# Two mixed layers on one core: a new order for the last group of the MLP, two transposes put inside other products, a halved last sigmoid, and gate sums one call earlier

## The chip, the cores and the metric

The kernel runs on one core of one Trainium2 chip. The metric is the device time of one execution in microseconds. The engines of the core work side by side, each through its own list of instructions in a fixed order: TensorE (PE in the profile; PEld is its weight load) does matrix products and transposes into PSUM banks, VectorE (DVE) and ScalarE (ACT) do elementwise work, GpSimd (POOL) does next to nothing here, and SyncE (SP) issues nearly all transfers between HBM and the on-chip memory; ScalarE's queue issues a few.

## The reference

A trunk of two layers on x of 512 tokens by 1024. Layer 0 mixes tokens with a Mamba-2 SSD block, layer 1 with HGRN2. What this text is about is the second half of each layer, which is the same in both:

```python
h = layer_norm(DEEPNORM_ALPHA * x + mix, ln_g[i, 0], ln_b[i, 0])
h = layer_norm(DEEPNORM_ALPHA * h + sq_relu_mlp(h, mlp_w1[i], mlp_w2[i]), ln_g[i, 1], ln_b[i, 1])
x = h + jax.nn.sigmoid(h @ ple_w_gate[i]) * (p[i] @ ple_w_proj[i])

def sq_relu_mlp(h, w1, w2):          # 1024 -> 4096 -> 1024
    a = jax.nn.relu(h @ w1)
    return (a * a) @ w2
```

`p[i]` is a 512 by 256 embedding of the layer, `ple_w_proj[i]` takes it to 1024, and the gate is a 1024 by 1024 product. All numbers are fp32.

## The kernel before

Each fp32 product is made of three matmuls (`mm3`, lines 120 to 122): every operand is split into a high part (a cast by ScalarE, tags `whi` for weights) and a low part (the rest, a subtraction by VectorE, `wlo`), and high x high, high x low and low x high are summed in PSUM. A weight of 128 by 1024 is loaded by SP into one of three `raw` buffers (`unit`), then split into one of six `whi` and six `wlo` buffers (`split`: L114 is the cast, L116 the subtraction).

`mlp_and_gate(layer, ...)` is the second half of a layer. It has two parts.

**The MLP** runs in five groups. A group g below 4 makes eight tiles T of the hidden layer, 128 hidden features each (`hidden`: 24 matmuls into a bank `pj`, then ReLU, L528, and a square of two tiles together, L530, into z tiles of the tags `a` and `b`). After every fourth tile `half_blocks` makes from them half of the contents of seven operands, `a11`, `a12`, `a22`, `s1` to `s4`: a cast by ScalarE (L357), a low half by VectorE (L358), and four sums and differences between them (L362 to L366). These seven are the left factors of a 2 by 2 block product in seven products instead of eight (`block_product`). So the second matrix of group g - 1 is applied in seven products Q of 24 matmuls while the tiles of group g are made. The order within groups is written by hand, one string for each group:

```python
PERIODS = ("TTTTTTTT",) + 3 * ("TTQTQTQTQTQTQTQ",) + ("QQQQQQQ",)
for op in period:
    next(tiles if op == "T" else products)
    if 0 < g < 4 and op == "Q":
        next(ahead, None)
```

The products of groups 1 to 3 come in the order a11, a12, s2, s3, s1, a22, s4; those of the last group, which works on the blocks of group 3, in the order a11, s3, s2, a22, s1, a12, s4, so that the first two token chunks (`c` 0 and 1) are complete after s1. The right factors for s1, s2, s3 and a22 are sums of weights, made by `weight_sums` in eight buffers `r`; those for the others come through `raw`. `s3` and `s4` have two buffers of the tag `blk`, the other five share nine of the tag `b8`. A product of 24 matmuls adds its two banks (`py` or `pj`) into `acc` by VectorE (L471, in the last group for some L467, which sums up the row for the norm too).

**The sums of the gate's weights** are made ahead, during groups 1 to 3 (`sums_ahead`): 20 pieces in four rounds of five. A round loads four blocks of 256 KB into one `whi` and one `wlo` buffer, makes four sums in two pieces, then casts and subtracts in two more, and writes the results to HBM (`pre`) from ScalarE's queue: the high parts from `sg` (L418), the low parts, which stand in the `whi` and `wlo` buffers themselves, from there (L425). The writes of low parts of a piece are issued at the next call. One call (`next(ahead)`) is made after each product.

**The end of the layer.** The norm of a chunk (`chunk`) is followed by `turned(c)`: eight transposes on TensorE into the banks `pt` and `pm` (L318), and copies from there by ScalarE (L308, L324, L326) with low halves by VectorE (L309), which are the left factors of the gate's product. `turned(0)` is put behind the last matmul of the MLP's last product (`turns` in `block_product`), `turned(1)` behind the first embedding product, `proj(0, 0)`, six matmuls of p by `ple_w_proj`; `proj(1, 0)` follows. The gate is again a block product in seven parts. `finish(c, h, sg)` multiplies the sigmoid by the embedding product (L611), adds it into `acc` (L612), both on VectorE, and in layer 1 writes the output (L614). The very last `finish` works on two halves of 256 columns; its sigmoid (L673) is one instruction of 512 columns.

**What sets the order of instructions.** In this part of the program a planner lays out each engine's list from the program's order, priorities (`tc.high_priority(offset=n)` lets instructions pass for n places earlier in the program) and its own estimate of when operands are ready; TensorE's matmuls of different products may so be interleaved. `tc.issue_after(ins)` (here `behind`) keeps instructions behind one that is named, on the same engine. Once laid out, an engine takes its list strictly in order, and an instruction that waits holds all that stand behind it.

Of the kernel before, what the change touches and what calls it, by code (L numbers as in the profile page):

```python
# [11 lines left out]
AF = mybir.ActivationFunctionType  # L12
# [16 lines left out]
SOON = 40  # L29
TURN = 200  # L30

PERIODS = ("TTTTTTTT",) + 3 * ("TTQTQTQTQTQTQTQ",) + ("QQQQQQQ",)
SUMS = (60, 300, 300, 300)

JOBS = "q0 q1 v0 q2 q3 g0 q4 q5 v1 q6 q7 g1 o".split()
# [6 lines left out]
def trunk(ctx: ExitStack, tc, a):  # L42
    nc = tc.nc
# [14 lines left out]
    uid, marks = [0], {}  # L58
# [41 lines left out]
    def behind(ins):  # L100
        return nullcontext() if ins is None else tc.issue_after(ins.ins)
# [17 lines left out]
    def mm3(out, sh, sl, mh, ml, start, stop, **kw):  # L119
        nc.tensor.matmul(out, sh, mh, start=start, stop=False, **kw)  # L120
        nc.tensor.matmul(out, sh, ml, start=False, stop=False, **kw)  # L121
        marks["pe"] = nc.tensor.matmul(out, sl, mh, start=False, stop=stop, **kw)  # L122
# [36 lines left out]
    with tc.high_priority(offset=FIRST):  # L159
# [7 lines left out]
        for k in range(8):  # L167
            hi, lo = (v[:, k % 4, :] for v in early[k // 4])
            x, w = slots[k][:, 0:T], slots[k][:, T:768]
# [266 lines left out]
            us.append((hi, lo))  # L436
        return us

    def block_product(w, blk, lead, first, after=None, turns=None, sums=None):

        with behind(marks.pop(("turned", 0), None) if first else None):
            t1, t2, t3, t4 = weight_sums(w, lead)
        seen = set() if first else {(i, j) for i in range(2) for j in range(2)}
        banks = {}

        def product(x, f, name, start, i, j, turns=None):
            us = [split(v) if f in (t1, t2, t3, t4) else unit(v) for v in f]
            if start:  # L450
                banks[name] = [bank(psy, "py%d" % c) if name == "x" else bank(psj, "pj") for c in range(2)]
            t = blk[x]
            for c in range(2):
                ps = banks[name][c]
                sl = slice(c * P, (c + 1) * P)
                for k in range(4):
                    hi, lo = us[k // 2]
                    ks = slice((k % 2) * 512, (k % 2 + 1) * 512)
                    w_ = hi[:, ks], lo[:, ks]
                    mm3(ps, t[:, 0, k, sl], t[:, 1, k, sl], *w_, start and k == 0, k == 3, skip_group_check=True)  # L460
                    if turns and (c, k) == (1, 3):
                        with behind(marks["pe"]):
                            turns()
                d = acc[:, 2 - 2 * i + c, j * 512 : (j + 1) * 512]
                with tc.high_priority(offset=SOON if after else 0):
                    if after and f in (w[1][0], t1, t4, w[1][1]):
                        marks["acc"] = nc.vector.tensor_tensor_reduce(  # L467
                            d, ps, d, 1.0, 0.0, ALU.add, ALU.add, sums[:, 2 - 2 * i + c, j : j + 1]
                        )
                    elif (i, j) in seen:  # L470
                        marks["acc"] = nc.vector.tensor_add(d, ps, d)  # L471
                    else:
                        marks["acc"] = nc.vector.scalar_tensor_tensor(d, d, ALPHA, ps, ALU.mult, ALU.add)
            seen.add((i, j))

        p1 = lambda: product("a11", w[0][0], "x", True, 0, 0)
        p2 = lambda: product("a12", w[1][0], "z", True, 0, 0)
        p6 = lambda: product("s2", t2, "x", False, 1, 0)
        p7 = lambda: product("s3", t3, "y", True, 1, 1)
        p5 = lambda: product("s1", t1, "x", False, 1, 1)  # L480
        p4 = lambda: product("a22", t4, "y", False, 1, 0)
        p3 = lambda: product("s4", w[1][1], "x", False, 0, 1, turns)
        for f in (p1, p7, p6, p4, p5, p2, p3) if after else (p1, p2, p6, p7, p5, p4, p3):
            f()
            if after and f is p5:
                after(0), after(1)
            if after and f is p3:
                after(2), after(3)
            yield

    def mlp_and_gate(layer, h_s, last, turns=()):

        w1, w2 = a[f"w1_{layer}"], a[f"w2_{layer}"]
        blocks = {}
# [44 lines left out]

        for g, period in enumerate(PERIODS):  # L540
            if g < 4:
                tiles = hidden(g)
            if g > 0:
                if g == 4:
                    blk, after, turned, sums, later = norm_blocks(2 * layer + 1)
                    p_s = (mk(w4, [P, 2, T], "a", F32R), mk(w4, [P, 2, T], "b", F32R))
                    praw = mk(raws, [P, 1024], "raw")
                    nc.sync.dma_start(praw, a[f"pT_{layer}"].rearrange("p k t -> p (k t)"))
                    praw = praw.rearrange("p (k t) -> p k t", k=2)
                    nc.scalar.copy(p_s[0], praw)  # L550
                    nc.vector.tensor_sub(p_s[1], praw, f32(p_s[0]))
                w = [[[w2[8 * g - 8 + 4 * i + 2 * j + u] for u in range(2)] for j in range(2)] for i in range(2)]
                products = block_product(w, blocks.pop(g - 1), SUMS[g - 1], g == 1, *((after, lambda: turned(0), sums) if g == 4 else ()))
            for op in period:
                next(tiles if op == "T" else products)
                if 0 < g < 4 and op == "Q":
                    next(ahead, None)
                if g == 4:
                    for _ in ahead:
                        pass  # L560
# [14 lines left out]

        pus, pps, held = {}, {}, {}

        def proj(c, h, parts=1):
            if h not in pus:
                pus[h] = unit(a[f"wp_{layer}"][h])  # L580
            pu = pus[h]
            pps[c, h] = []
            n = 512 // parts
            for i in range(parts):
                pp = bank(psj, "pj")[:, :n]
                for k in range(2):
                    ks = slice(k * 512 + i * n, k * 512 + (i + 1) * n)
                    mm3(pp, p_s[0][:, k, c * P : (c + 1) * P], p_s[1][:, k, c * P : (c + 1) * P], pu[0][:, ks], pu[1][:, ks], k == 0, k == 1)
                pps[c, h].append(pp)

        def product(x, f, c, ps, start, hook=()):
            cs = slice(c * P, (c + 1) * P)
            for k in range(4):
                hi, lo = f[k // 2]
                ks = slice((k % 2) * 512, (k % 2 + 1) * 512)
                mm3(ps, blk[x][:, 0, k, cs], blk[x][:, 1, k, cs], hi[:, ks], lo[:, ks], start and k == 0, k == 3, skip_group_check=True)
                for at in hook:
                    if (c, k) == at[:2]:
                        with behind(marks["pe"]):
                            turned(at[2])  # L600

        def finish(c, h, sg):
            with behind(marks["pe"]):
                while late:
                    late.pop(0)()
            pp = pps.pop((c, h))
            n = 512 // len(pp)
            for i, part in enumerate(pp):
                cs = slice(i * n, (i + 1) * n)
                d = acc[:, c, h * 512 + i * n : h * 512 + (i + 1) * n]  # L610
                nc.vector.tensor_mul(sg[:, cs], part, sg[:, cs])  # L611
                nc.vector.tensor_add(d, sg[:, cs], d)  # L612
                if last:
                    nc.sync.dma_start(a["out"][c * P : (c + 1) * P, h * 512 + i * n : h * 512 + (i + 1) * n], d)  # L614
            if not last:
                late.append(lambda: turn(h, c))

        two = lambda p, tag: [bank(p, tag % c if "%" in tag else tag) for c in range(2)]
        proj(0, 0)
        with behind(marks["pe"]):  # L620
            turned(1)
        proj(1, 0)
        xb = two(psy, "py%d")
        f = [unit(v) for v in wb[0][0]]
        for c in range(2):
# [3 lines left out]
        f = [unit(v) for v in wb[1][0]]  # L629
        for c in range(2):  # L630
            z = bank(psj, "pj")
            product("a12", f, c, z, True, ((1, 0, 2), (1, 3, 3)))
            sg = held[c]
# [4 lines left out]
        f = ready(pre, 2)  # L638
# [9 lines left out]
        f = ready(pre, 1)  # L648
# [4 lines left out]
        f = ready(pre, 3)  # L653
# [5 lines left out]
        f = ready(pre, 0)  # L659
# [7 lines left out]
        f = [unit(v) for v in wb[1][1]]  # L667
        for c in range(2):
            if c == 0:
                proj(0, 1)  # L670
            product("s4", f, c, xb[c], False)
            sg = tmp("sg", [P, T])
            nc.scalar.activation(sg, xb[c], AF.Sigmoid)  # L673
            if c:
                proj(1, 1, 2 if last else 1)
            finish(c, 1, sg)
        return x_n, late

# [3 lines left out]
    first = [bank(psy, "py0"), bank(psy, "py1")]  # L682
    for k in range(8):
        if k == 6:
            for i in range(8):
                for c in range(NCH):
# [4 lines left out]
                        start=i == 0,  # L691
# [3 lines left out]
        parts = [tuple(v[:, k % 4, i * P : (i + 1) * P] for v in early[k // 4]) for i in range(2)]  # L695
# [794 lines left out]
```

## Time and profile before

| | |
|---|---|
| median of 3 runs | 1412.51 us (1411.73 to 1412.81) |
| profiled execution | 1411.54 us |
| its span, first to last instruction | 1409.8 us |
| PE busy, PEld busy | 1400.4 us (99%), 1168.9 us (83%) |
| DVE, ACT, POOL busy | 1076.0 us (76%), 777.6 us (55%), 1.8 us |
| granted TensorE clock | 1.000 |

Matmuls are pipelined and their ends are modelled, so the busy time of PE hides short stops; a stop is better seen from the start of one matmul to the start of the next, or from the length of stretches of equal work. In a row such as `654.86 0.33 ACTq L425 ...` the first number is the start in us from the span's start, the second the duration; `L425` is the line of the kernel; `out<-in` gives the buffers' tags; what stands in brackets is the idle time of the engine before the instruction and what ended it. `ACTq` and `SPq` are issues of transfers by ScalarE and SyncE. In rows of stretches the columns are named in the header: length, then busy time and number of instructions for each engine, the granted clock (1.00 is full), the busy share of the DMA engines and GB/s.

### The profile page before, as it was taken

The numbers are of one execution on the slowest core, as the hardware profiler recorded it, in microseconds if no ns is written. First come the engines' busy times: TensorE is split into PE (matmuls) and PEld (weight loads), VectorE is DVE, ScalarE is ACT, GpSimd is POOL, SyncE is SP. The second block draws the span as 40 slices with busy tenths as digits, with TensorE's granted clock in tenths as the row PEclk, the third lists the DMA queues.
The fourth block names the chain that finished last, engine by engine and source line by source line (L and its number), as shares of the span: only waits on it lengthen the run. The fifth ranks groups of instructions, "written<-read, shape, count | busy, mean of one in ns | idle before, by whom it ended". The sixth has DMA issues, their size and how long they took to land.

```text
span 1409.8 us, 20492 instructions
## 1 busy us (share of the span) xinstructions
PE 1400.4 (99%) x7973; PEld 1168.9 (83%) x7973; DVE 1076.0 (76%) x1777; ACT 777.6 (55%) x1164; POOL 1.8 (0%) x11
## 2 busy tenths in 40 slices
PE   9999999999999999999999999999999999999998
PEld 7888888888988888887888888888898888888787
DVE  7997877696866878787985774776785877868986
ACT  7886666573554555545564446465454554544563
POOL 0000000000000000000000000000000000000000
PEclk9999999999999999999999999999999999999999
DMA  8423333323354646655473321222163566565364
GB/s 295 157 98 135 103 108 120 105 90 105 129 185 143 228 161 204 211 176 177 139 280 122 104 92 62 89 92 75 61 239 122 171 209 214 175 215 194 108 246 154
DMA packets 66819, 214.70 MB, mean 152 GB/s; under 512 B 7713, under 2 KB 8353, under 8 KB 66593
## 3 DMA queue, kind: packets, MB, share of 16 engines
q1 hardware_dynamic: 57504, 196.59, 41.6%
q10 hardware_dynamic: 9216, 16.78, 3.3%
q8 instruction: 63, 1.03, 0.3%
q14 instruction: 36, 0.29, 0.1%
HBM read 194.41 MB, written 18.94 MB: 151 GB/s over the span
## 4 chain that ended last, share of the span: by engine, by line
PE 96%; DMA 1%; DVE 1%; ACT 1%; issue 1%; SPq 0%; DVEq 0%; ACTq 0%
PE pj L120 25%; PE pj L122 24%; PE pj L121 24%; PE py L120 5%; PE py L122 5%; PE py L121 5%; PE py L881 1%; PE py L1147 1%; PE py L883 1%; DVE wlo L116 1%; PE pt L864 0%; DMA raw<-in_whvg 0%; DMA acc<-in_xw 0%; ACT whi L114 0%; DMA pre<-whi 0%
## 5 line engine op out<-in xcount | busy, mean ns | idle before, releaser
L116 DVE TENSOR_TENSOR wlo<-raw,whi 128x1024 fp32r<-128x1024 f32 x222 | 269.4, 1221 | 171.6 <-ACT whi L114 170.4
L114 ACT CAST whi<-raw 128x1024 fp32r<-128x1024 f32 x222 | 232.8, 1051 | 302.3 <-PE pj L121 157.5
L120 PE MATMUL pj<-b,whi 128*128 128x512 f32 (+1 forms) x1000 | 379.6, 380 | 0.0
L121 PE MATMUL pj<-b,whi 128*128 128x512 f32 (+1 forms) x1000 | 377.3, 377 | 0.0
L122 PE MATMUL pj<-b,wlo 128*128 128x512 f32 (+1 forms) x1000 | 377.3, 377 | 0.0
L122 PEld LDWEIGHTS pj<-b,wlo 128*128 128x128 f32 x1000 | 188.2, 188 | 34.8
L121 PEld LDWEIGHTS pj<-b,whi 128*128 128x128 f32 x1000 | 188.2, 188 | 34.2
L120 PEld LDWEIGHTS pj<-b,whi 128*128 128x128 f32 x1000 | 188.0, 188 | 34.1
L122 PE MATMUL pj<-whi,b 128*128 128x512 f32 x530 | 206.1, 389 | 0.0
L120 PE MATMUL pj<-whi,b 128*128 128x512 f32 x496 | 196.1, 396 | 0.0
L121 PE MATMUL pj<-wlo,b 128*128 128x512 f32 x496 | 193.2, 390 | 0.0
L114 ACT CAST whi<-r 128x1024 fp32r<-128x1024 f32 x64 | 67.2, 1053 | 96.6 <-PE pj L121 79.9
L122 PEld LDWEIGHTS pj<-whi,b 128*128 128x128 f32 x530 | 99.5, 188 | 20.7 <-DVE b L1342 0.2
L120 PEld LDWEIGHTS pj<-whi,b 128*128 128x128 f32 x496 | 93.2, 188 | 20.3 <-ACT k L1076 0.5
L121 PEld LDWEIGHTS pj<-wlo,b 128*128 128x128 f32 x496 | 93.2, 188 | 18.5
L120 PE MATMUL py<-whi,b 128*128 128x512 f32 x256 | 100.7, 393 | 3.1 <-ACT b L357 3.1
L122 PE MATMUL py<-whi,b 128*128 128x512 f32 x256 | 99.8, 390 | 0.0
L121 PE MATMUL py<-wlo,b 128*128 128x512 f32 x256 | 99.7, 389 | 0.0
L116 DVE TENSOR_TENSOR wlo<-r,whi 128x1024 fp32r<-128x1024 f32 x64 | 77.8, 1220 | 27.8 <-ACT whi L114 24.0
L120 PEld LDWEIGHTS py<-whi,b 128*128 128x128 f32 x256 | 48.0, 188 | 15.0 <-ACT b L357 3.9
L122 PEld LDWEIGHTS py<-whi,b 128*128 128x128 f32 x256 | 48.1, 188 | 10.1
L121 PEld LDWEIGHTS py<-wlo,b 128*128 128x128 f32 x256 | 48.1, 188 | 9.7
(374 smaller groups left out, 1934.1 us busy)
## 6 DMA issues: line engine op xcount, KB each, us to landing
raw<-in_w SPq DMA_DIRECT2D x112, 512.0 KB, 3.4
r<-in_w SPq DMA_DIRECT2D x64, 512.0 KB, 4.0
raw<-in_wssd SPq DMA_DIRECT2D x38, 512.0 KB, 3.6
a<-csd SPq DMA_DIRECT2D x16, 512.0 KB, 3.6
raw<-in_wso SPq DMA_DIRECT2D x16, 512.0 KB, 3.7
pre<-sg ACTq DMA_DIRECT2D x32, 256.0 KB, 3.0
whi<-pre SPq DMA_DIRECT2D x16, 512.0 KB, 5.3
wlo<-pre SPq DMA_DIRECT2D x16, 512.0 KB, 6.6
```

What stands on the lines that cost most here:

```text
L114: nc.scalar.copy(hi[:, :n], f)
L116: nc.vector.tensor_sub(lo[:, :n], f, f32(hi[:, :n]))
L120: nc.tensor.matmul(out, sh, mh, start=start, stop=False, **kw)
L121: nc.tensor.matmul(out, sh, ml, start=False, stop=False, **kw)
L122: marks["pe"] = nc.tensor.matmul(out, sl, mh, start=False, stop=stop, **kw)
L881: nc.tensor.matmul(yd[64 * r : 64 * r + 64, sl], xdt[:, c, r, :], m[:, r, sl], start=True, stop=c == 0)
L883: nc.tensor.matmul(yd[64 * r : 64 * r + 64, sl], pv[:, c - 1, r, :], ecs[:, r, (c - 1) * P : c * P], start=False, stop=True,)
L1147: nc.tensor.matmul(ps[r][32 * b : 32 * b + 32, base + n * c : base + n * c + n], kk[r][:, ts], moving(r, 4 * c + b), start=True, stop=True,)
```

## The change

- Group 3 is ordered `TTTQTQTQTQTQTQQ` instead of `TTQTQTQTQTQTQTQ`: three tiles come ahead of the first product, and the last two products stand together at the end, so the last tile comes ahead of the sixth product.
- In groups 1 to 3 one more call of `sums_ahead` is made, after the second tile of the group.
- `turned(0)` is issued after the third of the six matmuls of `proj(0, 0)`, and `turned(1)` after the third of `proj(1, 0)`; the parameter `turns` of `block_product` goes.
- The last sigmoid of layer 1 is made in two halves.
- The first half of the very last `finish` is added by GpSimd instead of VectorE. All other `finish` have one part and stay on VectorE.

```diff
-PERIODS = ("TTTTTTTT",) + 3 * ("TTQTQTQTQTQTQTQ",) + ("QQQQQQQ",)
+PERIODS = ("TTTTTTTT",) + 2 * ("TTQTQTQTQTQTQTQ",) + ("TTTQTQTQTQTQTQQ", "QQQQQQQ")
...
-                    if turns and (c, k) == (1, 3):
-                        with behind(marks["pe"]):
-                            turns()
...
-            for op in period:
+            for n, op in enumerate(period):
                 next(tiles if op == "T" else products)
-                if 0 < g < 4 and op == "Q":
+                if 0 < g < 4 and (op == "Q" or n == 1):
                     next(ahead, None)
...
-        def proj(c, h, parts=1):
+        def proj(c, h, parts=1, turn=None):
...
                     mm3(pp, p_s[0][:, k, c * P : (c + 1) * P], p_s[1][:, k, c * P : (c + 1) * P], pu[0][:, ks], pu[1][:, ks], k == 0, k == 1)
+                    if turn == c and k == 0:
+                        with behind(marks["pe"]):
+                            turned(c)
...
-                nc.vector.tensor_add(d, sg[:, cs], d)
+                (nc.vector if i == len(pp) - 1 else nc.gpsimd).tensor_add(d, sg[:, cs], d)
...
-        proj(0, 0)
-        with behind(marks["pe"]):
-            turned(1)
-        proj(1, 0)
+        proj(0, 0, turn=0)
+        proj(1, 0, turn=1)
...
-            nc.scalar.activation(sg, xb[c], AF.Sigmoid)
+            parts = 2 if last and c else 1
+            for i in range(parts):
+                cs = slice(i * 512 // parts, (i + 1) * 512 // parts)
+                nc.scalar.activation(sg[:, cs], xb[c][:, cs], AF.Sigmoid)
             if c:
-                proj(1, 1, 2 if last else 1)
+                proj(1, 1, parts)
             finish(c, 1, sg)
```

More of the change, by code (lines that the diff above doesn't have):

```diff
@@ L437, in ready, with block_product @@
         return us
-    def block_product(w, blk, lead, first, after=None, turns=None, sums=None):
+    def block_product(w, blk, lead, first, after=None, sums=None):
         with behind(marks.pop(("turned", 0), None) if first else None):
@@ L446, in block_product, with product @@
         banks = {}
-        def product(x, f, name, start, i, j, turns=None):
+        def product(x, f, name, start, i, j):
             us = [split(v) if f in (t1, t2, t3, t4) else unit(v) for v in f]
@@ L481, in block_product @@
         p4 = lambda: product("a22", t4, "y", False, 1, 0)
-        p3 = lambda: product("s4", w[1][1], "x", False, 0, 1, turns)
+        p3 = lambda: product("s4", w[1][1], "x", False, 0, 1)
         for f in (p1, p7, p6, p4, p5, p2, p3) if after else (p1, p2, p6, p7, p5, p4, p3):
@@ L552, in mlp_and_gate @@
                 w = [[[w2[8 * g - 8 + 4 * i + 2 * j + u] for u in range(2)] for j in range(2)] for i in range(2)]
-                products = block_product(w, blocks.pop(g - 1), SUMS[g - 1], g == 1, *((after, lambda: turned(0), sums) if g == 4 else ()))
-            for op in period:
+                products = block_product(w, blocks.pop(g - 1), SUMS[g - 1], g == 1, *((after, sums) if g == 4 else ()))
+            for n, op in enumerate(period):
                 next(tiles if op == "T" else products)
-                if 0 < g < 4 and op == "Q":
+                if 0 < g < 4 and (op == "Q" or n == 1):
                     next(ahead, None)
```

## The prediction

> **What bounds the kernel now.** I read the page first (busy shares), then the waits of TensorE, then equal stretches of the span beside each other, and last the instructions of ScalarE and VectorE in the two stretches that came out long.
>
> ```profile
> span 1409.8 us, 20492 instructions
> PE 1400.4 (99%) x7973; PEld 1168.9 (83%) x7973; DVE 1076.0 (76%) x1777; ACT 777.6 (55%) x1164; POOL 1.8 (0%) x11
> ```
>
> TensorE is the bound, and the change takes no matmul away. It can win only where TensorE stands still. Its waits by line:
>
> ```profile
> engine line waited for: us in total, times, longest us
> PE py L120 <- ACT b L357: 3.1, 2, 1.8
> PE pt L318 <- ACT b L324: 0.3, 1, 0.3
> ```
>
> L357 is the `copy` of `half_blocks`; its two waits, one in each layer, are what this change can reach, with L318 (`turned`); the list's other rows belong to the start of the program and to the next phase. Since matmul ends are modelled, I measure the loss by stretches of equal work. Rows 1 and 3: six tiles or products of 24 matmuls in the middle of group 3 of each layer. Rows 2 and 4: the six products from the last one of group 3 to the fifth of the last group.
>
> ```profile
> core 0: us, PE busy (x) PEld busy (x) DVE busy (x) ACT busy (x) POOL busy (x), PEclk, DMA share, GB/s
> 600.03:632.67 32.64, 32.64 (x146) 27.03 (x144) 27.68 (x31) 15.30 (x19) 0.00 (x0) 1.00 0.53 172
> 654.43:689.24 34.81, 33.58 (x146) 26.69 (x145) 29.75 (x41) 20.35 (x25) 0.00 (x0) 1.00 0.35 112
> 1251.98:1284.62 32.64, 32.64 (x145) 27.04 (x144) 27.58 (x31) 15.29 (x19) 0.00 (x0) 1.00 0.52 173
> 1306.38:1341.75 35.37, 33.50 (x146) 26.70 (x144) 30.32 (x42) 20.35 (x25) 0.00 (x0) 1.00 0.37 120
> ```
>
> The same 144 matmuls (the rest are neighbours cut by the edges) take 32.64 us undisturbed, so one operation of 24 takes 5.44 us and one matmul 0.227. The boundary loses 34.81 - 32.64 = 2.17 us in layer 0 and 35.37 - 32.64 = 2.73 in layer 1: 4.90 us together, at a granted clock of 1.00 in all four.
>
> Where it comes from, ScalarE and its own DMA issues, layer 0, then layer 1:
>
> ```profile
> 654.86 0.33 ACTq L425 DMA_DIRECT2D pre<-whi  x1
> 655.36 0.59 ACT L528 ACTIVATE b<-pj 128x512 f32<-128x512 f32 x1
> 655.98 1.06 ACT L530 ACTIVATE b<-b 128x1024 f32<-128x1024 f32 x1
> 658.96 2.00 ACT L114 CAST whi<-r 128x1024 fp32r<-128x1024 f32 x2 [1.92 <-DMA pre<-whi]
> 665.98 0.62 ACT L357 CAST b<-b 128x512 fp32r<-128x512 f32 x1 [2.51 <-DVE b L362]
> ...
> 1307.44 0.33 ACTq L425 DMA_DIRECT2D pre<-whi  x1
> 1311.53 2.00 ACT L114 CAST whi<-r 128x1024 fp32r<-128x1024 f32 x2 [2.54 <-DMA pre<-whi]
> ```
>
> The last tile T8 of group 3 is squared by 655.98 + 1.06 = 657.04. The next cast in ScalarE's order wants a `whi` buffer that the last piece of the gate sums is still writing to `pre`, and stands 1.92 us (2.54 in layer 1); the casts of T8's blocks are queued behind it, VectorE's low halves behind them. The `s3` block's second half comes out last:
>
> ```profile
> 668.27 0.68 DVE L358 TENSOR_TENSOR blk<-a,blk 128x512 fp32r<-128x512 f32 x1
> ...
> 1320.84 0.69 DVE L358 TENSOR_TENSOR blk<-a,blk 128x512 fp32r<-128x512 f32 x1
> ...
> 666.70 0.47 PE L120 MATMUL py<-whi,b 128*128 128x512 f32 x1 [1.23 <-ACT b L357]
> ```
>
> Without a stall, product a11 of the last group starts at 654.43 + 5.44 = 659.87, s3 at 665.31, and its second half of k six matmuls later, 666.67. Its low half is written at 668.95: 2.28 us late, against 2.17 lost. Layer 1: wanted at 1306.38 + 10.88 + 1.36 = 1318.62, written at 1321.53: 2.91 late, 2.73 lost. So the loss is the lateness of T8's blocks; the jumping ahead to ready halves of k (the 666.70 row) doesn't save it.
>
> **The change, part by part.**
>
> *The order of group 3.* Nothing is added. T8 changes places with the sixth product, so one more product, 5.44 us, stands between T8 and the s3 product. Against that: after T8, VectorE has that product's two accumulations more (2 x 0.69 = 1.4; an `acc<-py,acc` add is as long as the 0.69 row above), and its weights' casts come later. 5.44 - 2.28 - 1.4 = 1.8 us spare in layer 0, 1.1 in layer 1, before the hold is counted. The cover is the product itself; without it we are back at the loss. At the front of the group the first product waits for one more tile, whose blocks are older by then; the gate for `b8` buffers (`s2` of group 3 takes the one that `a11` of group 2 leaves) opens right before the fourth tile instead of before the third, and is wanted only after it. Weights on SP: two products in a row ask for two pairs of loads where a tile's single one stood between. The pair for Q6 is the `r` sums, the pair for Q7 `raw`; each is issued several operations ahead, so I take nothing. Ends: all of -4.90 to 0.
>
> *One more piece of the gate sums.* The generator has 20 pieces and a rest that only issues the last writes. Before, the rest came at the 21st call, at the last product of group 3: exactly the 654.86 write. With a call more in each group (8, 8, then) it comes at the fourth product of group 3, operation 10 of 15 instead of 15, and with it 4 loads of 256 KB on SP for each of the four rounds, the casts, VectorE's subtractions and ScalarE's writes. The hold of 1.92 and 2.54 leaves the boundary. That alone would leave 2.28 - 1.92 = 0.4 us late; with the other part, spare is 1.8 + 1.9 = 3.7 us, and 1.1 + 2.5 = 3.6 in layer 1. The price is paid elsewhere: the third round's writes move from the second product of group 3 to the last one of group 2, in front of the three tiles. Has such a hold cost TensorE anything elsewhere?
>
> ```profile
> 484.71 2.00 ACT L114 CAST whi<-raw 128x1024 fp32r<-128x1024 f32 x2 [2.85 <-DMA pre<-whi]
> 1137.36 2.00 ACT L114 CAST whi<-raw 128x1024 fp32r<-128x1024 f32 x2 [3.54 <-DMA pre<-wlo]
> 480.00:500.00 20.00, 20.00 (x90) 16.57 (x89) 15.28 (x20) 12.77 (x17) 0.00 (x0) 1.00 0.62 207
> 1130.00:1150.00 20.00, 20.00 (x90) 16.54 (x89) 15.79 (x20) 11.29 (x15) 0.00 (x0) 1.00 0.73 238
> ```
>
> Holds of 2.85 and 3.54 us, longer than those that hurt, and the 20 us around each hold 90 matmuls: 20 / 0.227 = 88 and the edges. Six weight buffers carry TensorE over them when no fresh block is wanted. Three tiles want none. Together these two edits: -4.90, which I take whole.
>
> *The turns.* `turned(0)` goes 3 matmuls (0.68 us) later, into the first embedding product; `turned(1)` into the second after its third matmul: six matmuls between the two now by program, nine in the trace. No instruction is added. What sets `turned(1)`:
>
> ```profile
> 700.76 0.58 ACT L308 CAST b<-pt 128x512 fp32r<-128x512 f32 x1 [4.83 <-PE pt L318]
> 701.92 1.05 ACT L114 CAST whi<-raw 128x1024 fp32r<-128x1024 f32 x1 [0.58 <-DMA raw<-in_wg]
> 702.88 0.58 ACT L324 COPY b<-pt 128x512 f32<-128x512 f32 x1
> 703.51 0.66 PE L318 MATMUL pt<-cst,acc 128*128 128x128 f32 x4 [0.26 <-ACT b L324]
> ```
>
> It needs the bank that L324 empties, and that copy stands behind a weight cast that waits for its load. `turned(0)` later makes L308 and so L324 later by up to 0.68; three matmuls remain to fill in. Ends: -0.3 (the wait gone) to +1.36 (0.68 shown in each layer). I take +0.4, nearer the first end, because the planner already puts embedding matmuls into that hole.
>
> *The tail.* VectorE's last four, ScalarE's last sigmoid, and the only rows that POOL and the output queue offer:
>
> ```profile
> 1404.36 0.60 ACT L673 ACTIVATE sg<-py 128x512 f32<-128x512 f32 x1 [2.12 <-PE py L122]
> 1405.14 0.42 DVE L611 TENSOR_TENSOR sg<-pj,sg 128x256 f32<-128x256 f32 x1 [1.46 <-PE pj L122]
> 1405.60 0.42 DVE L612 TENSOR_TENSOR acc<-sg,acc 128x256 f32<-128x256 f32 x1
> 1405.95 0.42 DVE L611 TENSOR_TENSOR sg<-pj,sg 128x256 f32<-128x256 f32 x1
> 1406.40 0.43 DVE L612 TENSOR_TENSOR acc<-sg,acc 128x256 f32<-128x256 f32 x1
> 1405.47 0.28 PE L122 MATMUL pj<-whi,b 128*128 128x256 f32 x1
> L1009 POOL MEMSET sc<- 128x512 f32 x2 | 1.0, 526 | 387.7 <-DVE b L309 387.7
> L614 SPq DMA_DIRECT2D out<-acc x9: 332/332/338, 1376.7 to 1406.9; - x9
> ```
>
> The halved sigmoid gains nothing: the whole one ends at 1404.96, and the first multiply waits for TensorE until 1405.14. The second multiply, freed of the add in front of it, can start when its matmuls end (1405.75, plus the 0.1 seen at the first) instead of 1405.95: -0.1 for the last write. But the first half's write, ahead of it on SP, now waits for POOL. The trace has no POOL add. Bounds from the memset: 0.31 us (half of 0.526 and some fixed part) to 0.94 (three streams instead of one). From 1405.62 it ends by 1405.9 to 1406.6; a 0.33 issue later SP is free at 1406.3 to 1406.9, the second write is due at 1406.75. So -0.1 to +0.1: 0. The Trainium skill ("GPSIMD Engine Reference", Elementwise — side-by-side cycle accounting) speaks against this edit: a two-input add takes POOL 1.96 times VectorE's time. By that rule, an estimate of 1.96 x 0.42 = 0.82 us, the add ends at 1406.44 and the tail also comes out at 0; no row here shows it.
>
> **The sum.** -4.9 + 0.4 + 0 = -4.5 us: a profiled execution of 1411.54 (span 1409.8 and 1.74 around it) becomes 1407.0. The median of the runs is 1412.51, 0.97 above the profiled one, so I forecast 1412.51 - 4.5 = 1408.0.
>
> **The rivals.**
>
> *VectorE takes over, half the loss stays.*
>
> ```profile
> 649.15:700.12 50.97, 49.74 (x217) 40.00 (x216) 44.22 (x64) 28.88 (x39) 0.00 (x0) 1.00 0.34 113
> ```
>
> From T8's end to the end of the last group VectorE is busy 44.22 of 50.97 us, 87%, and nine products now come in a row. Against it: the new stretch is 5.44 us longer and has only a product's 3.8 us (two low halves of 1.2, two adds of 0.69) more to do, with four gate subtractions fewer. If half stays: -2.2, 1410.3.
>
> *Nothing happens.* The block casts also stand behind casts for the next weights; if the planner keeps that order, T8's earliness is handed to those. For it: in the ScalarE rows the two weight casts of 658.96 go ahead of the blocks' casts. Against: they too wait for buffers that the sums no longer hold. 1412.5.
>
> *Slower: the write-back hold starves TensorE at the boundary of groups 2 and 3.* It lies in front of T1, with T8 of group 2 just done, the very pattern that hurts today. Price: at most the write from issue to landing, 1307.44 to 1311.53 = 4.1 us in each layer, 8.2. It decides from 2.25 us a layer on. Against it are the two stall-free stretches above, and no product follows for 16 us. All of it: 1412.5 - 4.5 + 8.2 = 1416.2.
>
> **How the numbers follow.** 0.2% of 1412.51, about what a measurement tells from no change here, is 2.8 us: faster is below 1409.7, slower above 1415.3. Forecast 0.67 (own range 1406.9 to 1409.4: the turns' and the tail's good ends, -4.9 - 0.3 - 0.1 and 0.3 of spread; and 1.4 more with the bad end of the turns), half 0.15, nothing 0.10, slower 0.08. Faster: the forecast but for 0.02, and 0.03 of the half case, 0.68. Slower: 0.08, and 0.01 from the others. The rest, 0.23, is the same. The range for 8 in 10 goes from 1406.8 to 1411.4, takes in the half case and leaves out nothing and slower.
>
> **What would show it.** Right: the wait of py on L357 is gone from TensorE's list, and the six products from the last of group 3 on take 32.7 us in both layers; the last `pre` write lies some 20 us ahead of T8's end (four operations); no wait above 0.3 us at the start of group 3. The turns: L318's wait between 0 and 1 us. The tail: POOL's add ends before 1406.5 on the old clock. Wrong: if TensorE shows new waits on `whi` or `wlo` in the nine products (VectorE), on a block in L357 again (nothing), or in the three tiles (slower).

## The result and the profile after

The changed kernel takes 1406.28 us in the median (1405.47 to 1406.87), beside 1412.81 for the kernel before in the same comparison (1411.73 to 1412.98): a ratio of 0.9956, 95% interval 0.9942 to 0.9969. Run again later, beside other runs of the kernel before, it took 1406.48 against 1412.38, the same 0.9956 (0.9943 to 0.9968). The forecast was 1408.0 and the range began at 1406.8: the direction was right, the gain of some 6 us was larger than the 4.5 forecast, and the time lies just below the range.

The head of the page of the kernel after, and TensorE's waits by line:

```profile
span 1403.8 us, 20493 instructions
...
PE 1397.9 (100%) x7973; PEld 1169.4 (83%) x7973; DVE 1076.3 (77%) x1776; ACT 775.9 (55%) x1165; POOL 2.5 (0%) x12
```

```profile
engine line waited for: us in total, times, longest us
PE pm L155 <- DVE y L152: 1.1, 1, 1.1
PE py L120 <- DVE acc L468: 0.5, 1, 0.5
PE py L120 <- ACT whi L174: 0.2, 1, 0.2
```

The two waits for a block's cast (3.1 us) and the wait of a transpose for its bank (0.3) are gone. One wait of 0.5 us for an accumulation is new: VectorE has come in a little way behind ScalarE.

To place the rest I cut both traces at the same matmuls. In the next two fences (before, then after; the columns are those of the stretches in the prediction) rows 1 and 3 run from the first matmul of group 3's last product to the first matmul of the last group's last product, that is seven operations, 7 x 5.44 = 38.1 us undisturbed; call them the boundary of layer 0 and of layer 1. Rows 2 and 4 run on from there, in layer 0 to the next layer's first matmul, in layer 1 to the program's last one; they hold the turns.

```profile
654.43:694.68 40.25, 39.02 (x170) 31.19 (x169) 34.92 (x52) 25.09 (x35) 0.00 (x0) 1.00 0.36 118
694.68:762.90 68.22, 67.75 (x329) 55.51 (x328) 57.38 (x84) 38.24 (x65) 1.05 (x3) 1.00 0.64 222
1306.38:1347.19 40.81, 38.94 (x170) 31.21 (x168) 35.56 (x55) 25.18 (x35) 0.00 (x0) 1.00 0.38 123
1347.19:1405.47 58.28, 58.28 (x278) 48.37 (x277) 45.06 (x68) 28.56 (x50) 0.00 (x0) 1.00 0.58 213
```

```profile
653.71:692.55 38.84, 38.38 (x170) 31.45 (x168) 33.36 (x52) 21.73 (x31) 0.00 (x0) 1.00 0.30 99
692.55:759.84 67.29, 67.29 (x329) 55.59 (x328) 57.03 (x82) 38.14 (x64) 1.05 (x3) 1.00 0.65 225
1303.28:1341.49 38.21, 38.21 (x170) 31.45 (x168) 32.72 (x50) 21.61 (x30) 0.00 (x0) 1.00 0.28 96
1341.49:1399.52 58.03, 58.03 (x279) 48.39 (x277) 45.02 (x68) 28.34 (x51) 0.00 (x0) 1.00 0.60 213
```

The span fell by 1409.8 - 1403.8 = 6.0 us: 1.41 and 2.60 in the two boundaries, 0.93 and 0.25 behind them, and 0.72 ahead of the first boundary (its start moves from 654.43 to 653.71). Of that, 0.69 is there after 15 us, ahead of any edit; over the fourteen profiles of this text the same matmul starts anywhere from 653.38 to 654.43. The tail, from the last matmul's start to the end of the span, is 1409.8 - 1405.47 = 4.3 us and 1403.8 - 1399.52 = 4.3 us.

### The profile page after: what moved, and what is told of

It is laid out like the page before. It is cut to its first block, busy times and chain, and to the rows that moved or that the text cites. A ratio compares the mean times of both kernels' runs of the same rounds, so it can differ in the third digit from the quotient of the medians.

```text
span 1403.8 us, 20493 instructions
## 1 busy us (share of the span) xinstructions
PE 1397.9 (100%) x7973; PEld 1169.4 (83%) x7973; DVE 1076.3 (77%) x1776; ACT 775.9 (55%) x1165; POOL 2.5 (0%) x12
## 4 chain that ended last, share of the span: by engine, by line
PE 96%; DVE 2%; DMA 1%; ACT 1%; issue 0%; SPq 0%; DVEq 0%; ACTq 0%
PE pj L120 24%; PE pj L122 24%; PE pj L121 24%; PE py L120 5%; PE py L122 5%; PE py L121 5%; PE py L882 1%; PE py L1148 1%; PE py L884 1%; DVE wlo L116 1%; DMA r<-in_w 1%; PE pt L865 0%; DMA acc<-in_xw 0%; PE pt L226 0%; PE pt L825 0%; PE pt L1317 0%
```

## The experiments

The four parts, each alone on the kernel before. The edits are those lines of the diff above that belong to the part.

**The order alone.**

```diff
-PERIODS = ("TTTTTTTT",) + 3 * ("TTQTQTQTQTQTQTQ",) + ("QQQQQQQ",)
+PERIODS = ("TTTTTTTT",) + 2 * ("TTQTQTQTQTQTQTQ",) + ("TTTQTQTQTQTQTQQ", "QQQQQQQ")
```

> The kernel before with only the new order of group 3. Measured by the boundary, the stretch from the first matmul of group 3's last product to the first matmul of the last group's last product (seven products, 38.1 us if nothing stands still; before 40.25 in layer 0 and 40.81 in layer 1; the changed kernel 38.84 and 38.21). Theory A (what counts is how late the last tile's blocks are written): 5.44 us more lead is more than the 2.28 and 2.91 they were late, so the boundary falls to 38.1 to 38.9 in both layers and the time by about 4 us. Rival B (the hold of ScalarE behind the gate sums' last write is the cause, wherever the tile stands): the last call is still at the last product, the hold stays, the boundary stays above 39.5 in both layers, the time falls by less than 1.5 us.

Measured: 1418.10 us (1417.34 to 1419.86) beside 1412.32, ratio 1.0040 (1.0026 to 1.0054). By itself the order costs 5.8 us. Its waits of TensorE, VectorE's rows ahead of the first of them, and four stretches: the boundary of layer 0, then three around the wait:

```profile
PE py L120 <- DVE acc L471: 7.4, 2, 3.7
```

```profile
661.75 0.70 DVE L358 TENSOR_TENSOR blk<-a,blk 128x512 fp32r<-128x512 f32 x1
662.35 0.69 DVE L358 TENSOR_TENSOR blk<-b,blk 128x512 fp32r<-128x512 f32 x1
662.95 2.36 DVE L116 TENSOR_TENSOR wlo<-r,whi 128x1024 fp32r<-128x1024 f32 x2
665.22 0.70 DVE L420 TENSOR_TENSOR whi<-whi,sg 128x512 fp32r<-128x512 f32 x1
665.82 0.70 DVE L420 TENSOR_TENSOR wlo<-wlo,sg 128x512 fp32r<-128x512 f32 x1
666.42 1.23 DVE L116 TENSOR_TENSOR wlo<-r,whi 128x1024 fp32r<-128x1024 f32 x1
667.56 1.29 DVE L471 TENSOR_TENSOR acc<-py,acc 128x512 f32<-128x512 f32 x2
```

```profile
653.84:698.49 44.65, 40.95 (x169) 33.17 (x168) 36.05 (x54) 23.70 (x34) 0.00 (x0) 0.92 0.35 125
658.00:664.60 6.60, 6.60 (x29) 4.92 (x27) 6.60 (x10) 5.87 (x8) 0.00 (x0) 1.00 0.39 131
668.31:673.50 5.19, 5.19 (x12) 4.13 (x13) 4.01 (x5) 0.78 (x1) 0.00 (x0) 0.50 0.12 40
673.60:679.00 5.40, 5.40 (x25) 4.46 (x24) 3.49 (x4) 2.11 (x2) 0.00 (x0) 1.00 0.12 49
```

The blocks are in good time now: the low half `blk<-a,blk`, of s3, begins at 661.75, where before it began at 668.27. But VectorE makes blocks, weights' low halves and gate pieces in one unbroken row, and the accumulations that empty the banks `py` stand behind all of it. The matmul that needs such a bank waits 3.7 us, until 668.31, in layer 1 as well. And the stop has a second price: the 12 matmuls after it come at a granted clock of 0.50, against 1.00 ahead of the stop and 5.2 us later. So a boundary of 44.65 us instead of 38.1 is 3.7 us of stop, some 12 x 0.2 = 2.4 us of slow matmuls (they start 0.43 us apart instead of 0.227), and crumbs.

**The gate sums' piece alone.**

```diff
-                if 0 < g < 4 and op == "Q":
+                if 0 < g < 4 and (op == "Q" or n == 1):
```

> The kernel before with only one more call of the gate sums in each of groups 1 to 3. The hold of 1.92 and 2.54 us leaves the boundary, the last tile stays where it was. Theory A: late by 2.28 - 1.92 = 0.4 and 2.91 - 2.54 = 0.4 us, boundary 38.4 to 38.8 in both layers, time down by about 4 us: each of the two edits alone would do most of it. Rival B (hold alone): the same here. Rival C (the order does it; with the hold gone another wait in the same queue takes its place, the next buffers being still in use): boundary above 39.5, time down by less than 1.5 us.

Measured: 1406.20 us (1405.16 to 1406.85), ratio 0.9954 (0.9941 to 0.9966). The boundaries of this kernel, and ScalarE in the first:

```profile
654.32:692.54 38.22, 38.22 (x169) 31.43 (x168) 32.91 (x51) 24.49 (x34) 0.00 (x0) 1.00 0.28 97
1303.50:1341.71 38.21, 38.21 (x169) 31.42 (x168) 32.89 (x51) 24.48 (x34) 0.00 (x0) 1.00 0.29 97
```

```profile
655.87 1.06 ACT L530 ACTIVATE b<-b 128x1024 f32<-128x1024 f32 x1
656.97 1.14 ACT L357 CAST b<-b 128x512 fp32r<-128x512 f32 x2
658.60 1.06 ACT L114 CAST whi<-r 128x1024 fp32r<-128x1024 f32 x1 [0.49 <-PE py L122]
```

This one line is the boundary's whole gain; nothing is left of the loss. The casts of T8's blocks now follow the square at once. Counted from the stretch's start they begin at 656.97 - 654.32 = 2.65 us; in the kernel before the first began after the hold and two weight casts,

```profile
660.87 0.61 ACT L357 CAST blk<-b 128x512 fp32r<-128x512 f32 x1
```

or 660.87 - 654.43 = 6.44 us from the start. Earlier by 3.8 us, not by the hold's 1.92 alone.

**The turns alone, the tail alone.**

> The kernel before with only the two transposes moved into the embedding products. Measured from the first matmul of the last group's last product to the next phase's first matmul (layer 0: before 68.2 us, changed kernel 67.3) and to the program's last matmul (layer 1: 58.3, changed 58.0). What I predicted: 0.2 us longer in each. Theory D, from the changed kernel's trace (the turns are the reason of the gain there): 67.3 and 58.0, time down by 1.2 us, the boundary unchanged at 40.2 and 40.8. Rival E (the gain there is a consequence of the earlier parts, buffers and weights arriving in another order): 68.2 and 58.3, time the same.

> The kernel before with only the halved last sigmoid and the first half's last add on GpSimd. From the end of the last matmul to the end of the span: 4.0 us before and 4.0 in the changed kernel. Expected 4.0 within 0.1, all else as before, and no change of time; if GpSimd's add (0.72 us in the changed kernel) delayed the writes, 4.2 to 4.4.

Measured: turns 1411.53 us (1409.69 to 1413.67), ratio 0.9995 (0.9986 to 1.0004); tail 1412.48 (1410.56 to 1414.6), 0.9999 (0.9990 to 1.0007). Neither tells from no change. In the kernel with the turns the stretches behind the boundary took 67.42 and 58.03 us, much as in the changed kernel; in the one with the tail, the tail took 4.3 us as before. Both show the old loss in a new size, though no edit touches the boundary: 42.73 and 40.93 us in the kernel with the turns, 41.00 and 42.50 in the one with the tail, against 40.25 and 40.81. What sets the size is visible. Layer 0 of the kernel with the turns, then of the one with the tail:

```profile
660.07 2.00 ACT L114 CAST whi<-r 128x1024 fp32r<-128x1024 f32 x2 [2.58 <-DMA pre<-whi]
...
667.80 0.77 PE L120 MATMUL py<-whi,b 128*128 128x512 f32 x1 [2.67 <-ACT b L357]
```

```profile
658.65 2.01 ACT L114 CAST whi<-r 128x1024 fp32r<-128x1024 f32 x2 [2.66 <-DMA pre<-whi]
...
666.39 0.47 PE L120 MATMUL py<-whi,b 128*128 128x512 f32 x1 [1.97 <-ACT b L357]
```

Take the end of ScalarE's hold, counted from the start of the boundary, and subtract TensorE's stop. Turns: 660.07 - 654.09 - 2.67 = 3.31. Tail: 658.65 - 653.38 - 1.97 = 3.30. Before: 658.96 - 654.43 - 1.23 = 3.30. Layer 1 gives 3.30, 3.32 and 3.31 in the same way. Over six boundaries with stops of 1.23 to 2.67 us the stop follows the end of the hold one for one: where these writes to `pre` stand just ahead of T8's blocks, the end of the hold, which is their landing, sets the stop.

**The write's hold taken away, its place kept.** In the kernel before, the very last pair of low parts is written to `pre` from the `sg` buffers of the high parts, so that no `whi` or `wlo` buffer is held by it:

```diff
-                        lows.append((dst[n, u, 1][:, cs], f32(x)))
+                        lows.append((dst[n, u, 1][:, cs], f32(hi) if u == h == 1 and pair[0][0] == 0 else f32(x)))
```

> The kernel before, with one thing changed: the very last pair of low parts that the gate sums write (second column half, second unit) is written from the buffer of the high parts instead, so the weight buffers are free before the write. Same calls, same number and size of writes; that quarter of two low parts then holds the high parts' numbers. Theory A' (ScalarE's hold behind that write is the cause): boundary at most 39 us in both layers instead of 40 to 43, time 4 to 6 us down. Rival N (not the hold but the last pieces' work on ScalarE and VectorE at this place): boundary above 40 in both, time down by less than 1.5.

Measured: 1410.38 us in the median, ratio 0.9986 (0.9977 to 0.9995); ten executions took 1408.27 to 1411.55, an eleventh 2861.52, which nothing here explains. Only 1.7 us come back: the boundaries are 40.07 and 40.50 us. That is near what rival N expected, and far from theory A'.

```profile
655.61 1.06 ACT L114 CAST whi<-r 128x1024 fp32r<-128x1024 f32 x1 [2.15 <-DVE whi L420]
655.62 0.33 ACTq L425 DMA_DIRECT2D pre<-sg  x1
```

```profile
PE pj L120 <- ACT blk L357: 1.6, 2, 0.8
PE py L120 <- DVE acc L471: 1.1, 3, 0.5
```

The next weight cast waits 2.15 us all the same, now for the subtraction L420 that makes the low part in the `whi` buffer. Once the landing is gone, the piece's own work is next in line. What had to go from this place was the piece, not only its write.

**One call earlier instead of three.** How far must it go? One more call in group 3 alone (after its second tile) puts the last writes one product ahead, in front of T8's tile:

```diff
-                if 0 < g < 4 and op == "Q":
+                if 0 < g < 4 and (op == "Q" or (g, n) == (3, 1)):
```

> The kernel before with one more call of the gate sums in group 3 alone (after its second tile), none in groups 1 and 2: the last computed piece and the last writes come one product earlier than in the kernel before (writes at the sixth product instead of the seventh, just ahead of the last tile), against three products earlier in the change. Theory R (what hurts is the sums' last writes and casts standing right ahead of the last tile's blocks; a product's and a tile's length, 10.9 us, is more than the write's 4.1 us): the whole gain, 38.2 to 38.6 us for the seven operations in both layers, 1406.2 to 1407 us. Rival S (the sums' work itself, casts and subtractions, crowds ScalarE and VectorE up to the last tile, so the gain grows with the distance): part of it, 39 to 40 us in each layer, 1408 to 1410.5.

Measured: 1406.92 us (1406.06 to 1408.13), ratio 0.9960 (0.9947 to 0.9974), the changed kernel on the same chip 1406.48.

```profile
653.80:692.05 38.25, 38.25 (x169) 31.44 (x168) 33.90 (x51) 24.39 (x34) 0.00 (x0) 1.00 0.34 113
1303.24:1341.48 38.24, 38.24 (x169) 31.44 (x168) 34.46 (x53) 24.54 (x35) 0.00 (x0) 1.00 0.35 119
```

One product's distance empties both boundaries as well as three do (38.22). So it is a matter of place, not of how much work crowds the two engines.

**The order with VectorE's adds put earlier.** If the order fails by VectorE's list, moving the accumulations of group 3's products forward in it must help:

```diff
-                with tc.high_priority(offset=SOON if after else 0):
+                with tc.high_priority(offset=SOON if after else soon):
...
-                products = block_product(w, blocks.pop(g - 1), SUMS[g - 1], g == 1, *((after, lambda: turned(0), sums) if g == 4 else ()))
+                products = block_product(w, blocks.pop(g - 1), SUMS[g - 1], g == 1, *((after, lambda: turned(0), sums) if g == 4 else ()), soon=TURN if g == 3 else 0)
```

> The kernel with only the new order of group 3 (44.6 us in both boundaries, 5.8 us slower than before) plus an earlier place for VectorE's adds of group 3's products (priority 200 places ahead). Theory L (with two products in a row at the end, the last product's adds stand in VectorE's list behind the last tile's blocks and the gate's last piece, so TensorE waits for its bank): boundary below 41 in both layers, time below 1412. Rival M (the adds only show the delay; ScalarE's hold behind the gate's writes is what delays all): boundary stays above 43.

Measured: 1407.87 us (1407.52 to 1408.42) beside 1412.05 before, ratio 0.9968 (0.9956 to 0.9981): from 5.8 us slower to 4.2 faster, without moving the gate sums.

```profile
653.47:693.00 39.53, 38.36 (x169) 31.45 (x168) 37.22 (x57) 24.55 (x35) 0.00 (x0) 1.00 0.50 165
1303.82:1343.15 39.33, 38.33 (x169) 31.46 (x168) 36.98 (x57) 24.23 (x35) 0.00 (x0) 1.00 0.47 160
```

```profile
PE py L120 <- DVE acc L471: 2.2, 2, 1.2
```

The boundary falls from 44.65 to 39.5 and 39.3; the rest is the same wait, shorter. The last writes of the gate sums still stand in the boundary (issued from 669.54 in layer 0), so it is not they that cost the order alone its 5.8 us: VectorE's list is the cause, shown.

**The change without the new order.** Run on two chips:

> The changed kernel with the order of group 3 as before (gate sums, turns and tail changed). Where the time comes from, by the runs so far: the gate sums alone take all the boundary's loss (38.2 us in both layers), the turns 0.9 and 0.25 us at the layers' ends. Theory H (the order adds nothing once the sums are early, and costs the 0.6 us that TensorE stands for VectorE's add in layer 0): boundary 38.2 in both, ends 67.3 and 58.0 as in the changed kernel, 0.5 to 1 us faster than the changed kernel, about 1405.4. Rival (the order is needed for the turns' gain, or the boundary reopens with the turns): boundary above 39 in one layer, or 1406.3 and more.

> The changed kernel with the old order of group 3, again, beside the changed kernel. Theory M (the new order does nothing of the gain; with the sums' piece in place it only leaves a residual wait of 0.62 us in layer 0): 38.2 us in both layers, some 0.6 us faster than the changed kernel, 1405.5 to 1405.9. Rival N (the order does help, at other places of the program): equal to the changed kernel or slower, 1406.3 or more.

Measured: 1405.49 us (1404.52 to 1406.39), 0.9951 (0.9938 to 0.9963), and 1405.58 (1405.03 to 1405.76), 0.9950 (0.9938 to 0.9963), the second beside 1406.48 (1404.92 to 1406.81) for the changed kernel on the same chip. It is the fastest median of all and needs one edit less, but the ranges overlap, so that 0.9 us is likely and not settled. The profiles don't show where it would come from: the boundaries are 38.2 us in both layers of both runs.

> The changed kernel itself, on the chip on which the next three run, so that they can be compared with it directly. Both theories: 1406.3 us, ratio 0.9956 to the kernel before; the six products from the last of group 3 on, measured as the seven operations from its first matmul to the first matmul of the last group's last product (7 x 5.44 = 38.1 us undisturbed), 38.8 us in layer 0 and 38.2 in layer 1 as in the first profile.

In that second profile the changed kernel shows 38.2 us in both boundaries, not 38.8 in layer 0: the residual wait of 0.5 us is not always there.

**Where that residual comes from.** In the change, the load of the embedding `p` and its split are moved from the beginning of the last group to behind its third product, since that load holds a `raw` buffer for long (in the changed kernel it is issued at 632.2 and cast at 659.7 us):

```diff
                 next(tiles if op == "T" else products)
+                if g == 4 and n == 2:
...
+                    nc.sync.dma_start(praw, a[f"pT_{layer}"].rearrange("p k t -> p (k t)"))
...
+                    nc.scalar.copy(p_s[0], praw)
+                    nc.vector.tensor_sub(p_s[1], praw, f32(p_s[0]))
```

> The changed kernel with the embedding's load and split written two products later in the last group, so that it takes no raw buffer while the last products' weights are loaded. The changed kernel's layer 0 has one wait left at the boundary (38.84 us instead of 38.2), TensorE behind VectorE's add of the last product. Theory J (the weights' loads are late for want of a raw buffer, ScalarE stands behind them, VectorE with it): boundary of layer 0 at 38.2 to 38.4. Rival K (the add stands too far back in VectorE's list, whatever the loads): 38.7 to 38.9 as before.

Measured: 1405.98 us (1405.52 to 1406.61), ratio 0.9955 (0.9942 to 0.9967), boundaries of 38.20 and 38.17. One ScalarE row of the changed kernel and the same of this one:

```profile
649.15 1.05 ACT L114 CAST whi<-raw 128x1024 fp32r<-128x1024 f32 x1 [2.79 <-DMA raw<-in_w]
```

```profile
648.87 1.05 ACT L114 CAST whi<-raw 128x1024 fp32r<-128x1024 f32 x1 [2.10 <-PE pj L121]
```

With the residual, a weight cast waits for its load; without it, for TensorE as usual. The second profile of the changed kernel has no wait for that load and no residual; the kernel without the turns (below) has both, 2.92 us and a boundary of 38.85. So in these four profiles the residual goes together with a late load, and it comes in some executions only. That the later load of `p` cures it is not shown, since the changed kernel is without it at times too.

**The change without the turns.**

> The changed kernel with turned(0) and turned(1) at their old places; order, sums' piece and tail as changed. Theory O (the turns gain a little: the wait of turned(1) for its bank is gone when it stands in the second embedding product): 0.3 to 0.5 us slower than the changed kernel, the stretch from the last product's first matmul to the next phase some 67.5 in layer 0 and 58.2 to 58.3 in layer 1, against 67.3 and 58.0. Rival P (the prediction's +0.4: the turns cost): 0.4 us faster than the changed kernel. Rival Q (the turns do nothing): within 0.1 us.

Measured: 1406.23 us (1404.97 to 1407.66), ratio 0.9957 (0.9945 to 0.9970), the changed kernel 1406.48 beside it. The stretches behind the boundary:

```profile
692.73:760.22 67.49, 67.49 (x330) 55.58 (x328) 57.07 (x82) 38.23 (x64) 1.05 (x3) 1.00 0.66 225
...
1341.87:1400.12 58.25, 58.25 (x279) 48.38 (x277) 45.08 (x68) 28.69 (x52) 0.00 (x0) 1.00 0.60 212
```

0.20 and 0.22 us longer than with the turns moved (67.29, 58.03). Over all profiles the same stretches took 67.27 to 67.42 and 58.02 to 58.06 in the six with the turns moved, 67.33 to 68.22 and 58.13 to 58.34 in the eight without. The turns are worth a few tenths; the medians can't tell that much. Theory O's reason is not shown: the kernel without the turns has no wait of L318 in TensorE's list either. Only its weight loads (PEld) at L318 still stand idle, 0.8 us for L324 in both layers together, against 0.4 for L326 in the changed kernel.

## Where the prediction was right, and where it failed

**What bounds, and where.** Right. The loss lay in the lateness of T8's blocks at the boundary, the wait on L357 is gone, and both layers now run at the undisturbed rate, but for the residual of layer 0 in some executions.

**The order's 5.44 us against 2.28 + 1.4.** This step failed, and it is the largest error of the reasoning. It didn't show in the forecast by luck: the two edits were priced together, and the other one takes the whole loss away by itself. I charged VectorE for two accumulations more and found 1.8 and 1.1 us spare "before the hold is counted". Alone, the order makes the kernel 5.8 us slower. The sum asked when the blocks would be ready; it didn't ask where the accumulations would stand in VectorE's list once nine products come in a row and a bank is wanted every half product. My rival "VectorE takes over" named the right engine and argued it away by its busy share over 51 us; the 3.7 us stop comes from the order inside 7 us of its list (the rows from 661.75 to 668.85), while over the boundary VectorE is busy 36.05 of 44.65 us. The sign that I set for this rival, waits on `whi` or `wlo`, would have missed it: the wait is for an accumulation, L471.

**The sums' piece alone would leave 0.4 us late.** Failed, to the good: it leaves nothing (38.22 and 38.21 us). I priced it by the idle time in the bracket, 1.92 us. But in the kernel before two weight casts, 2.00 us, also went ahead of the blocks; with the piece moved they don't, and the blocks' casts come 3.8 us earlier. With 2.28 us of lateness that is cover enough without any new order.

**The size, -4.9.** This step put the forecast too high by 1.4 us, and the turns (below) by another 0.8: the mechanism was right, the term too small. The boundaries' 40.25 + 40.81 = 81.06 us were read from one execution. Two more kernels with the same boundary show 42.73 + 40.93 = 83.66 and 41.00 + 42.50 = 83.50. Against 2 x 38.2 = 76.4 the loss is 4.7, 7.3 and 7.1 us, 6.3 on average. I noticed that the profiled execution was 0.97 us below the median and added that to the forecast as an offset that the change would leave. More likely it belonged to the loss: the three profiled executions with losses of 4.7, 7.3 and 7.1 us took 1411.54, 1412.66 and 1412.48 us. Three executions argue this, they don't show it. With the 0.97 in the gain the forecast would have been 1407.0. With 6.3 us for the boundaries and -0.4 for the turns the sum gives 1412.51 - 6.7 = 1405.8, 0.5 below what was measured.

**The turns, +0.4.** Wrong sign: about -0.2 in each layer. The delay that I feared, up to 0.68 us in each, doesn't come. Why there is a small gain instead stays open.

**The tail, 0.** Right, and for the reason given: POOL's add is hidden, and the second write sets the end. Of the kernel after, around the end:

```profile
1399.19 0.42 DVE L611 TENSOR_TENSOR sg<-pj,sg 128x256 f32<-128x256 f32 x1 [1.46 <-PE pj L122]
1399.69 0.72 POOL L612 TENSOR_TENSOR acc<-sg,acc 128x256 f32<-128x256 f32 x1 [672.68 <-DVE sg L611]
1399.91 0.42 DVE L611 TENSOR_TENSOR sg<-pj,sg 128x256 f32<-128x256 f32 x1 [0.29 <-PE pj L122]
1400.37 0.43 DVE L612 TENSOR_TENSOR acc<-sg,acc 128x256 f32<-128x256 f32 x1
```

The add takes 0.72 us, inside the bounds of 0.31 to 0.94, and ends at 1400.41, ahead of VectorE's half at 1400.80. By the Trainium skill ("GPSIMD Engine Reference", Elementwise — side-by-side cycle accounting) it was estimated at 0.82 us, 1.96 times VectorE's; here it is 0.72 / 0.42 = 1.7 times, and by either value the tail is the same within 0.1 us.

**The slower rival**, a write-back hold that starves TensorE at the boundary of groups 2 and 3: refuted. The writes were moved as forecast, the last one to 1277.7, 26 us ahead of the second boundary:

```profile
L425 ACTq DMA_DIRECT2D pre<-wlo x16: 326/326/625, 459.3 to 1277.7; - x16
```

No wait of TensorE is left from them: from the last product of group 1 to that of group 3 both traces of layer 0 take 163.2 us (491.23 to 654.43 before, 490.51 to 653.71 after).

## What to carry to other kernels

When a buffer is held by an outgoing write, price the place of the write by what the engine's list does behind it: the idle time in the bracket was only half here, the work that went in front was the other. Before an order is changed, walk each engine's list around the spot, bank-emptying adds included; a busy share over a long stretch says nothing of a stop of 4 us. And a loss that hangs on a transfer's landing differs from execution to execution: read it in more than one profile, or let the gap between the profiled execution and the median widen the gain, not shift the forecast.

## What the runs showed of the hardware

A stop of TensorE can cost more than itself by way of the clock. Stops of 1.23 to 1.97 us (the kernel before; the turns alone, layer 1; the tail alone, layer 0) left the granted clock at 1.00. After 2.32 us (the tail alone, layer 1), 2.67 us (the turns alone, layer 0) and 3.7 us (the order alone, both layers) it fell. The tail alone, layers 0 and 1 and a stretch around the stop at 1318.90; then the turns alone, layer 0 and a stretch behind its stop at 667.80:

```profile
653.38:694.38 41.00, 38.99 (x170) 31.21 (x169) 35.47 (x53) 25.08 (x35) 0.00 (x0) 1.00 0.38 123
1305.53:1348.03 42.50, 40.18 (x170) 32.45 (x168) 36.26 (x55) 25.20 (x35) 0.00 (x0) 0.96 0.37 123
1318.00:1330.00 12.00, 11.10 (x41) 8.76 (x42) 10.67 (x16) 7.49 (x9) 0.00 (x0) 0.86 0.01 2
```

```profile
654.09:696.82 42.73, 40.06 (x170) 32.51 (x168) 36.26 (x53) 25.11 (x36) 0.00 (x0) 0.96 0.36 116
669.00:674.00 5.00, 5.00 (x19) 3.97 (x19) 4.60 (x7) 2.73 (x5) 0.00 (x0) 0.80 0.00 0
```

In the order alone the matmuls ran at 0.50 for some 5 us. The stop of 1.97 us made its boundary 41.00 - 38.2 = 2.8 us too long, 0.8 more than itself, and so did the shorter stops within 0.1; the one of 2.32 us made its own 42.50 - 38.2 = 4.3 too long, 2.0 more than itself. So where the clock fell after a stop of 2.3 us, that cost some 1.2 us. These few stops don't place a threshold: after the one of 2.32 us the matmuls kept their full rate for another 1.5 us and slowed down only from 1320.45 on. The Trainium skill ("TensorE: Matmul & The Clock Gate", What's actually happening) puts the fall to half rate after an idle window of about 3.4 us that runs free of the program; half rate agrees with the 0.50, while here a stop of 2.32 us was enough.
